# Softmax times V on one core: stores moved from SyncE's queue to GpSimd's, and the cast of V from GpSimd to VectorE

## The chip, the cores and the metric

The kernel runs on one core of one Trainium2 chip. A core has five engines that this text names by the profile's letters: PE (TensorE, matrix products, with PEld for its weight loads), DVE (VectorE), ACT (ScalarE), POOL (GpSimd) and SP (SyncE, which here only issues DMAs). Sixteen DMA engines move data between the chip's memory (HBM) and the core's on-chip memory (SBUF). The metric is the device time of one execution in microseconds (us); lower is better.

## The reference

For each of 8 x 12 = 96 heads there is a 1024 x 1024 float32 matrix of scores and a 1024 x 64 float32 matrix v. Softmax is taken along each row of the scores, and the result is multiplied by v.

```
batch, n_heads, seq, head_dim = 8, 12, 1024, 64
scores_max = np.max(scores, axis=-1, keepdims=True)
attn = np.exp(scores - scores_max)
attn = attn / (np.sum(attn, axis=-1, keepdims=True) + 1e-8)
return np.matmul(attn, v).astype(np.float32)
```

Of one head the scores are 4096 KB, v is 256 KB and the output is 256 KB.

## The kernel before, in words

A head is laid over 128 partitions: partition p holds 8 consecutive rows of the scores (R = 8, index r), 8 consecutive rows of v (C = 8, index c) and, later, 8 consecutive rows of the output. So a partition's share of a head is one run of 32 KB of scores, 2 KB of v and 2 KB of output in HBM.

The loop over heads n does this:

- `load(n)` issues two DMAs on SP: v into `v_sb` (L115), and the scores into `s_nat` (L120). The last head's scores come in four pieces of two rows each (1024 KB), all others in one piece. `v_pool` and `s_pool` have AHEAD = 4 buffers each. Loads of heads 0 to 3 are issued before the loop; `load(n + 4)` is issued in head n at r = 7 (L147).
- At the start of head n the 128 x 512 float32 `v_sb` is cast to float16 into one of three buffers `vones` (L130), on POOL. Each row of `vones` has a 65th element of 1.0, so that the same matrix product also gives the row sums of the softmax.
- For every second r, ACT takes the exponential of two rows per partition, 128 x 2048, from `s_nat` into the float16 tile `p_nat` (L136, four instructions for a head). No maximum is subtracted.
- For every r, PE transposes eight 128 x 128 blocks of `p_nat` into the PSUM tile `psT` (L140), and DVE copies that to SBUF as `pt` (L146).
- `finish` runs two r later (LAG = 2): eight matrix products of `pt` and `vones` add up in `psO` (L77, three PSUM buffers, each for four r). After four r, DVE takes the reciprocals of the row sums (L88) and multiplies (L89) into the tile `out_sb`, of which `ob_pool` has three. After r = 7 the head's `out_sb` goes to HBM in one DMA (L96), on SP.

All DMAs that SP issues are chained by `queue`, which makes the order of issue on SP that of the program's text: load of v, load of the scores, store, and so on. In the written order, the store of head n - 1 comes after `load(n + 3)` and before `load(n + 4)`. The order of instructions on the other engines is set by the framework's planner, which need not keep the written order: in the profile, both multiplications of L89 of a head come after that head's second reciprocal. The framework also puts in all waits.

Of the kernel before, what the change touches and what calls it, by code (L numbers as in the profile page):

```python
# [1 line left out]

# [5 lines left out]

FP32 = mybir.dt.float32
FP16 = mybir.dt.float16  # L10
EXP = mybir.ActivationFunctionType.Exp


@with_exitstack
def kernel(
    ctx: ExitStack,
    tc: tile.TileContext,
    scores: bass.AP,
    v: bass.AP,
    out: bass.AP,  # L20
):
    nc = tc.nc
    P = 128

    B, H, SQ, SK = scores.shape
    Bv, Hv, SKv, D = v.shape
    assert (B, H, SK) == (Bv, Hv, SKv)
    BH = B * H
    assert SQ % P == 0 and SK % P == 0
    R = SQ // P  # L30
    C = SK // P
    M = D + 1
    EB = 2
    G = 4
    LAG = 2
    NV = 3
    AHEAD = 4

    sc_bh = scores.rearrange("b h (p r) j -> (b h) p r j", p=P)
    v_bh = v.rearrange("b h (p c) d -> (b h) p c d", p=P)
    out_bh = out.rearrange("b h (p r) d -> (b h) p r d", p=P)

    const_pool = ctx.enter_context(tc.tile_pool(name="const", bufs=1))
    s_pool = ctx.enter_context(tc.tile_pool(name="spool", bufs=AHEAD))
    p_pool = ctx.enter_context(tc.tile_pool(name="ppool", bufs=6))
    v_pool = ctx.enter_context(tc.tile_pool(name="vpool", bufs=AHEAD))
    pt_pool = ctx.enter_context(tc.tile_pool(name="ptpool", bufs=5))
    ob_pool = ctx.enter_context(tc.tile_pool(name="obpool", bufs=3))  # L50
    rc_pool = ctx.enter_context(tc.tile_pool(name="rcpool", bufs=4))
    psT_pool = ctx.enter_context(tc.tile_pool(name="psTp", bufs=5, space=bass.MemoryType.PSUM))
    psO_pool = ctx.enter_context(tc.tile_pool(name="psOp", bufs=3, space=bass.MemoryType.PSUM))

    ident32 = const_pool.tile([P, P], FP32, name="ident32")
    make_identity(nc, ident32)
    ident16 = const_pool.tile([P, P], FP16, name="ident16")
    nc.vector.tensor_copy(out=ident16[:], in_=ident32[:])  # L58


    vones_bufs = []
    for k in range(NV):
        vo = const_pool.tile([P, C, M], FP16, name=f"vones{k}")
        nc.vector.memset(vo[:, :, D : D + 1], 1.0)  # L64
        vones_bufs.append(vo)

    pending = []

    def finish(u):

        n, r, pt, st = u
        g = r % G
        if g == 0:
            st["psO"] = psO_pool.tile([P, G, M], FP32, tag="psO", name="psO")
        psO = st["psO"]
        for c in range(C):
            nc.tensor.matmul(  # L77
                out=psO[:, g, :],
                lhsT=pt[:, c * P : (c + 1) * P],
                rhs=st["vones"][:, c, :],  # L80
                start=(c == 0),
                stop=(c == C - 1),
            )
        if g == G - 1:
            if r == G - 1:
                st["out_sb"] = ob_pool.tile([P, R, D], FP32, tag="out_sb", name="out_sb")
            recip = rc_pool.tile([P, G, 1], FP32, tag="recip", name="recip")
            nc.vector.reciprocal(out=recip[:], in_=psO[:, :, D : D + 1])  # L88
            nc.vector.tensor_tensor(  # L89
                out=st["out_sb"][:, r - G + 1 : r + 1, :],  # L90
                in0=psO[:, :, 0:D],
                in1=recip[:].to_broadcast([P, G, D]),
                op=mybir.AluOpType.mult,
            )
        if r == R - 1:
            queue(nc.sync.dma_start(out=out_bh[n], in_=st["out_sb"][:]))  # L96

    queued = []

    def queue(dma):  # L100

        if queued:
            tc.add_manual_dep(
                dma.ins,
                queued[-1].ins.name,
                mybir.DependencyInfo(mybir.DependencyClass.NoSync, mybir.DependencyReason.DATA),
                reason="queue order",
            )
        queued.append(dma)

    loaded = {}

    def load(n):
        v_sb = v_pool.tile([P, C, D], FP32, tag="v_sb", name="v_sb")
        queue(nc.sync.dma_start(out=v_sb[:], in_=v_bh[n]))  # L115
        s_nat = s_pool.tile([P, R, SK], FP32, tag="s_nat", name="s_nat")
        step = EB if n == BH - 1 else R
        for r in range(0, R, step):
            queue(
                nc.sync.dma_start(out=s_nat[:, r : r + step, :], in_=sc_bh[n, :, r : r + step, :])  # L120
            )
        loaded[n] = (s_nat, v_sb)

    for n in range(min(AHEAD, BH)):
        load(n)

    for n in range(BH):
        s_nat, v_sb = loaded.pop(n)
        vones = vones_bufs[n % NV]
        nc.gpsimd.tensor_copy(out=vones[:, :, 0:D], in_=v_sb[:])  # L130
        st = dict(vones=vones)

        for r in range(R):
            if r % EB == 0:
                p_nat = p_pool.tile([P, EB, SK], FP16, tag="p_nat", name="p_nat")
                nc.scalar.activation(out=p_nat[:], in_=s_nat[:, r : r + EB, :], func=EXP)  # L136
            p_row = p_nat[:, r % EB, :].rearrange("p (q c) -> p c q", c=C)
            psT = psT_pool.tile([P, SK], FP16, tag="psT", name="psT")
            for c in range(C):
                nc.tensor.transpose(  # L140
                    out=psT[:, c * P : (c + 1) * P],
                    in_=p_row[:, c, :],
                    identity=ident16[:],
                )
            pt = pt_pool.tile([P, SK], FP16, tag="pt", name="pt")
            nc.vector.tensor_copy(out=pt[:], in_=psT[:])  # L146
            if r == R - 1 and n + AHEAD < BH:  # L147
                load(n + AHEAD)
            pending.append((n, r, pt, st))
            if len(pending) > LAG:  # L150
                finish(pending.pop(0))
    while pending:
        finish(pending.pop(0))


# [1 line left out]
_INS = ['scores', 'v']  # L157
_OUTS = [((8, 12, 1024, 64), 'float32')]


# [23 lines left out]
```

## Time and profile before

| | |
|---|---|
| median of 3 runs | 1090.23 us (1089.81 to 1090.62) |
| profiled execution | 1090.23 us, its span 1088.4 us |
| mean granted TensorE clock | 0.813 |
| PE, PEld busy | 782.8 us (72%), 743.7 us (68%) |
| ACT busy | 704.0 us (65%) |
| DVE busy | 628.2 us (58%) |
| POOL busy | 60.1 us (6%), of which 59.4 us in 96 casts of L130 |
| read from and written to HBM | 427.82 MB and 25.17 MB, 416 GB/s over the span |

The span is the time from the first instruction to the last; the time of an execution is longer by 1.83 us. In the rows of a timeline the columns are the start in us from the span's start, the time in us, the engine, the line, the operation with its tiles and shapes, the number of instructions that are merged into the row, and in brackets the idle time ahead and what ended it. SPq is SP's queue of DMA issues: a row of it is an issue, not a transfer. In a table of windows each row is a stretch of time with the busy time of each engine, the granted clock, the mean busy share of the 16 DMA engines and the GB/s that they moved. The page's lines DMA and GB/s cut the span into 40 equal slices.

### The profile page before, as it was taken

How to read it: one execution, taken by the hardware profiler on the slowest of the kernel's cores; microseconds unless marked ns; L12 is line 12 of the kernel's file. 1: busy time of each engine (PE TensorE's matmuls, PEld its weight loads, DVE VectorE, ACT ScalarE, POOL GpSimd, SP SyncE). 2: the span in 40 equal slices, each digit the busy share in tenths (PEclk: the TensorE clock that was granted, in tenths of full speed). 3: DMA queues.
4: the chain of work that ended last, by engine and by line, in shares of the span. 5: the costliest groups of instructions: out<-in, count | busy, mean ns of one | idle time of the engine just before them, and what ended most of it. 6: DMA issues, size and time to landing. Idle time of an engine off the chain costs nothing.

```text
span 1088.4 us, 27687 instructions
## 1 busy us (share of the span) xinstructions
PE 782.8 (72%) x12288; PEld 743.7 (68%) x12288; DVE 628.2 (58%) x1156; ACT 704.0 (65%) x385; POOL 60.1 (6%) x102
## 2 busy tenths in 40 slices
PE   3767777676777767677776767777676777767676
PEld 3667667676766767677676767677676767767676
DVE  2556556565555655556565655655565565556555
ACT  4667576666757666665766666575665757566675
POOL 0000000000000000000000000000000000000000
PEclk9888878778787877878888887878888787787888
DMA  9999999999999999999999999999999999999994
GB/s 396 423 430 425 423 423 427 427 426 428 427 422 423 424 431 427 422 426 424 431 425 429 425 426 424 425 429 428 424 423 430 424 426 427 428 420 428 426 398 160
DMA packets 42024, 454.77 MB, mean 418 GB/s; under 512 B 4656, under 2 KB 4656, under 8 KB 29232
## 3 DMA queue, kind: packets, MB, share of 16 engines
q1 hardware_dynamic: 41904, 453.00, 98.5%
q8 instruction: 96, 1.57, 0.6%
q14 instruction: 24, 0.20, 0.0%
HBM read 427.82 MB, written 25.17 MB: 416 GB/s over the span
## 4 chain that ended last, share of the span: by engine, by line
DMA 96%; DVE 1%; PE 1%; issue 0%; SPq 0%; ACT 0%; DVEq 0%; ACTq 0%
DMA out_dram<-out_sb 69%; DMA s_nat<-in_scores_dram 18%; DMA v_sb<-in_v_dram 9%; DVE out_sb L89 1%; PE psT L140 1%; PE psO L77 0%; SPq L120 0%; ACT p_nat L136 0%; DVE pt L146 0%; SPq L115 0%; DVE recip L88 0%; DVEq L89 0%; SPq L96 0%; ACTq L136 0%
## 5 line engine op out<-in xcount | busy, mean ns | idle before, releaser
L136 ACT ACTIVATE p_nat<-s_nat 128x2048 f16<-128x2048 f32 x384 | 702.8, 1901 | 375.8 <-DMA s_nat<-in_scores_dram 364.7
L140 PE MATMUL psT<-ident,p_nat 128*128 128x128 f16 x6144 | 621.6, 264 | 274.5 <-ACT p_nat L136 273.5
L140 PEld LDWEIGHTS <-p_nat 128*128 128x128 f16 x6144 | 524.9, 155 | 301.5 <-ACT p_nat L136 295.2
L146 DVE COPY pt<-psT 128x1024 f16<-128x1024 f16 x768 | 529.0, 691 | 307.2 <-PE psT L140 285.4
L77 PE MATMUL psO<-vones,pt 128*128 128x65 f16 x6144 | 343.0, 204 | 27.3 <-DVE pt L146 26.3
L77 PEld LDWEIGHTS <-pt 128*128 128x128 f16 x6144 | 295.4, 107 | 39.2 <-DVE pt L146 38.3
L89 DVE TENSOR_TENSOR out_sb<-psO,recip 128x256 f32<-128x256 f32 x192 | 73.6, 420 | 98.7 <-DMA out_dram<-out_sb 98.6
L130 POOL CAST vones<-v_sb 128x512 f16<-128x512 f32 x96 | 59.4, 619 | 1007.3 <-DMA v_sb<-in_v_dram 995.5
L88 DVE RECIPROCAL recip<-psO 128x4 f32<-128x4 f32 x192 | 34.1, 178 | 49.9 <-PE psO L77 49.9
L136 ACT ACT_TABLE_LOAD x1 | 1.3, 1283 | 0.7 <-PEq L168 0.7
L64 DVE MEMSET vones<- 128x8 f16 x3 | 0.1, 65 | 0.8 <-PEq L168 0.8
L58 DVE CAST ident<-ident 128x128 f16<-128x128 f32 x1 | 0.2, 227 | 0.4 <-POOL ident masks.py:199 0.4
masks.py:199 POOL TENSOR_SCALAR_AFFINE_SELECT ident<-ident 128x128 f32<-128x128 f32 x1 | 0.3, 294 | 0.1
masks.py:197 POOL MEMSET ident<- 128x128 f32 x1 | 0.2, 205 | 0.3 <-POOLq L168 0.3
L168 POOL MEMSET const-float32-0.0<- 128x1 f32 x1 | 0.1, 99 | 0.2 <-issue 0.2
L168 POOL MEMSET const-bfloat16-1.0<- 128x1 bf16 x1 | 0.1, 102 | 0.0
L168 POOL MEMSET const-uint8-127<- 128x1 uint8 x1 | 0.1, 102 | 0.0
L168 POOL MEMSET const-float32-1.0<- 128x1 f32 x1 | 0.1, 99 | 0.0
## 6 DMA issues: line engine op xcount, KB each, us to landing
s_nat<-in_scores_dram SPq DMA_DIRECT2D x95, 4096.0 KB, 32.5
v_sb<-in_v_dram SPq DMA_DIRECT2D x96, 256.0 KB, 23.5
out_dram<-out_sb SPq DMA_DIRECT2D x96, 256.0 KB, 32.4
s_nat<-in_scores_dram SPq DMA_DIRECT2D x4, 1024.0 KB, 23.8
```

Source lines behind the costliest of these rows:

```text
L58: nc.vector.tensor_copy(out=ident16[:], in_=ident32[:])
L64: nc.vector.memset(vo[:, :, D : D + 1], 1.0)
L77: nc.tensor.matmul(out=psO[:, g, :], lhsT=pt[:, c * P : (c + 1) * P], rhs=st["vones"][:, c, :], start=(c == 0), stop=(c == C - 1),)
L88: nc.vector.reciprocal(out=recip[:], in_=psO[:, :, D : D + 1])
L89: nc.vector.tensor_tensor(out=st["out_sb"][:, r - G + 1 : r + 1, :], in0=psO[:, :, 0:D], in1=recip[:].to_broadcast([P, G, D]), op=mybir.Al ...
L130: nc.gpsimd.tensor_copy(out=vones[:, :, 0:D], in_=v_sb[:])
L136: nc.scalar.activation(out=p_nat[:], in_=s_nat[:, r : r + EB, :], func=EXP)
L140: nc.tensor.transpose(out=psT[:, c * P : (c + 1) * P], in_=p_row[:, c, :], identity=ident16[:],)
L146: nc.vector.tensor_copy(out=pt[:], in_=psT[:])
L168: nc = _bacc.Bacc("TRN2", target_bir_lowering=False, num_devices=1)
```

## The change

Two lines differ. The store of a head is issued by GpSimd instead of SP, and it is no longer part of the chain that `queue` makes, which now holds loads alone. The cast of v into `vones` is done by VectorE instead of GpSimd.

```
@@ finish @@
         if r == R - 1:
-            queue(nc.sync.dma_start(out=out_bh[n], in_=st["out_sb"][:]))
+            nc.gpsimd.dma_start(out=out_bh[n], in_=st["out_sb"][:])
...
@@ loop over heads @@
     for n in range(BH):
         s_nat, v_sb = loaded.pop(n)
         vones = vones_bufs[n % NV]
-        nc.gpsimd.tensor_copy(out=vones[:, :, 0:D], in_=v_sb[:])
+        nc.vector.tensor_copy(out=vones[:, :, 0:D], in_=v_sb[:])
         st = dict(vones=vones)
```

## The prediction

> **What bounds the kernel now.** I read the page's slices first, then the chain, then the timelines of ACT and SP, which show the chain's meaning.
>
> ```profile
> PE   3767777676777767677776767777676777767676
> DMA  9999999999999999999999999999999999999994
> GB/s 396 423 430 425 423 423 427 427 426 428 427 422 423 424 431 427 422 426 424 431 425 429 425 426 424 425 429 428 424 423 430 424 426 427 428 420 428 426 398 160
> q8 instruction: 96, 1.57, 0.6%
> ```
>
> The DMA engines are busy in every slice but the last and move 420 to 431 GB/s throughout, while no compute engine is above 72%. The chain of waits seems to say something else: it gives 69% of the span to the stores.
>
> ```profile
> DMA out_dram<-out_sb 69%; DMA s_nat<-in_scores_dram 18%; DMA v_sb<-in_v_dram 9%; DVE out_sb L89 1%; PE psT L140 1%; PE psO L77 0%; SPq L120 0%; ACT p_nat L136 0%; DVE pt L146 0%; SPq L115 0%; DVE recip L88 0%; DVEq L89 0%; SPq L96 0%; ACTq L136 0%
> ```
>
> ```profile
> DVE out_sb L89 <- DMA out_dram<-out_sb: 98.6, 91, 2.6
> ```
>
> A store takes 32.4 us from issue to landing because it stands behind about three heads of loads on SP's queue; the multiplications of L89 wait for the store three heads back to free its tile. That is a loop of waits which ends just in time, on engines with slack; the DMA engines work all the while. So taking this wait away (98.6 us of DVE idle time) is worth nothing by itself. What counts is how long a head takes on the DMA engines, and ACT's starts show it, since ACT starts a head when its scores land:
>
> ```profile
> 13.55 7.32 ACT L136 ACTIVATE p_nat<-s_nat 128x2048 f16<-128x2048 f32 x4 [11.54 <-DMA s_nat<-in_scores_dram]
> 23.94 7.32 ACT L136 ACTIVATE p_nat<-s_nat 128x2048 f16<-128x2048 f32 x4 [3.07 <-DMA s_nat<-in_scores_dram]
> ...
> 101.66 7.33 ACT L136 ACTIVATE p_nat<-s_nat 128x2048 f16<-128x2048 f32 x4 [3.71 <-DMA s_nat<-in_scores_dram]
> 112.67 7.32 ACT L136 ACTIVATE p_nat<-s_nat 128x2048 f16<-128x2048 f32 x4 [3.68 <-DMA s_nat<-in_scores_dram]
> 124.97 5.52 ACT L136 ACTIVATE p_nat<-s_nat 128x2048 f16<-128x2048 f32 x3 [4.99 <-DMA s_nat<-in_scores_dram]
> ```
>
> Heads 0 and 1 were issued before any store: 23.94 - 13.55 = 10.39 us for 4.456 MB, 429 GB/s. Later heads carry one store each: 112.67 - 101.66 = 11.01 us. A store on SP's queue therefore costs 0.62 us, 423 GB/s: its bytes at the common rate, no more. The next head took 12.30 us, 1.29 more; such steps come about every eight heads and I take them for the instruction packets of q8 (96 packets of 16 KB, 1.09 us each by their share of 0.6% of 16 x 1088.4 us), which another queue feeds. The end:
>
> ```profile
> 1043.38 0.33 SPq L115 DMA_DIRECT2D v_sb<-in_v_dram  x1
> 1044.10 11.26 SPq L120 DMA_DIRECT2D s_nat<-in_scores_dram  x4
> 1055.68 29.90 SPq L96 DMA_DIRECT2D out_dram<-out_sb  x5
> ```
>
> ```profile
> 1066.02 14.54 ACT L136 ACTIVATE p_nat<-s_nat 128x2048 f16<-128x2048 f32 x8 [4.24 <-DMA s_nat<-in_scores_dram]
> ```
>
> ```profile
> PE psO L77 <- DVE out_sb L89: 1.0, 1, 1.0
> ```
>
> The five last stores (91 to 95) are issued after all loads. Head 94's scores land at 1066.02; from there ACT runs heads 94 and 95 without a gap, and the span ends 22.4 us later.
>
> **The change, part by part.** I sum against the profiled execution, 1090.23 us (span 1088.4, 1.83 around it), which is also the median.
>
> *Issue of loads.* SP's waits show that each DMA waits for the landing of the one eight issues earlier: in a head, L115 waited for scores (89 times), L120 for a store (89), L96 for a v load (79). With three DMAs a head, eight are 2.7 heads in flight; with loads alone they would be four, until the buffers (AHEAD = 4) bind: the next scores go out when ACT has finished with a buffer, 7.3 us after a landing. Either way two heads or more, over 20 us of work, are always queued, so the DMA engines gain no work: 0 us. If that depth were gone, each head would pay the issue-to-start time; nothing in the change takes it away.
>
> *The cast.* 96 casts leave POOL, where each took 0.619 us, off the path (POOL waited 995.5 us for v). On DVE the nearest row is the 128x128 float32 cast, 0.227 us; four times the elements lies between 0.23 and 0.91 us, and I take 0.6. That is 96 x 0.6 = 58 us more for DVE, from 628 to 686 of 1088 us, or 7.1 us of 11.2 a head. Its place: v of head n + 1 lands 0.7 to 1.4 us after the scores of head n, while DVE has nothing until PE's first transposes of head n, 3.1 us after that landing (copy at 307.28, scores at 304.17). The cast is done by then: 0 us. Behind a waiting cast are the copies of L146, and PE waits for those; without this cover a late cast would move a head's work back, which four buffers of scores absorb, except at the end (rival 4). The next load of v waits for the cast now on DVE; 256 KB, two heads ahead, free.
>
> *The stores.* 96 issues leave SP (0.33 us each, in waiting time) and go to POOL, which has no other work left. (a) Order. On SP, the loads of head 94 have 90 stores ahead of them (0 to 89; then 90, then 91 to 95 after the last load). On its own queue, store n starts as soon as its head is done, about when the next head's scores land, and shares the engines with the load after that. So stores 90 to 92 now move before head 94 has landed, and the bound stream is three stores longer: 3 x 0.62 = +1.86 us. They used to move when the engines ran half empty. (b) The end. PE's single wait of 1.0 us for L89 (a `psO` buffer held because `out_sb` waited for store 91, queued behind the last loads) goes away: -1.0 us. What is late next is PE itself. (c) The last store is issued by POOL. No DMA of POOL is in the trace. From the last multiplication's end (1085.22) to the span's end are 3.2 us with SP; with POOL I bound the difference by 0 and 3.2 (twice as slow) and take one POOL operation, 0.6, as its software may need about that to start: +0.6 us. (d) The price of a store while another queue's loads run. This is the term that decides, and the trace doesn't hold it. Nearest rows: 0.62 us from ACT's starts (the store's tail under the next load), and 0.67 us from SP's: at 1021.11 the scores have landed, at 1021.77 and likewise at 304.84 (after 304.17) the store has, so 0.66 to 0.67 if its completion isn't covered. Far ends: 0 us, if a store out of SBUF could run entirely beside loads into SBUF; and 0.62 + 0.68, if switching queues costs what a q8 packet does (1.29 us for 16 KB, which is 0.61 at the common rate; one store is also 16 KB on each engine). Those give -59 and +65 us. I take the middle of the two near rows, 0.645, since the interleaved store has the same shape and bytes: 96 x 0.025 = +2.4 us.
>
> Sum: 1.86 - 1.0 + 0.6 + 2.4 = +3.9 us, so 1094.1 us.
>
> The Trainium skill, *DMA: Bandwidth & Descriptors*, section "Issuing engines are not separate DMA queues", says that DMAs of all issuing engines share the same 16 DMA engines and interleave, so that several issuers save only issue time. By it (d) would be 0 and the sum +1.5 us, 1091.7 us; no run here has yet shown two large queues at once.
>
> A rule that speaks against the change stands in *SBUF — State Buffer*, section "SBUF: two separate sides": GpSimd makes its own descriptors, through a port pair that VectorE locks while it copies from SBUF to SBUF in a fast mode. Here 768 of DVE's copies read PSUM, and the moved cast is the only such copy; by the rule a store would be held up by one cast at most, and with three `out_sb` tiles the sum is the same.
>
> **The rivals.** 1. *Two queues fill each other's gaps: faster.* If a share of each store runs beside the loads, a quarter say, a store costs 0.465 us: -14.9 + 1.5 gives 1076.8 us. It decides from a price below 0.58 us, where 96 x 0.04 = 3.7 us outweigh the 1.5 and the 0.2%. For it: 429 GB/s need not be the ceiling. Against: the rate with stores in the stream (11.01 us for 4.719 MB, 429 GB/s) equals that without, so mixing directions brought nothing. 2. *Switching is dear: much slower.* For it the q8 packets, 1.29 us for 0.61 us of bytes. If a store pays a tenth to a half of that surplus, 0.07 to 0.34 us, that is +6.5 to +33 us on the 1.5: 1098 to 1125 us. Against: those packets go to another place than HBM. 3. *It does nothing measurable*: price exactly 0.62, a POOL issue as quick as SP's, the ends cancel: 1090.2 to 1091.7 us. That the DMAs stay in effect in one stream is part of it. 4. *The cast lands in the wrong place in DVE's order*, a head early, and DVE stalls for a v that has not come: the loads go on, but at the end up to one head of PE work (782.8 / 96 = 8.2 us) is left over: up to 1102 us. Against: L89's place in before shows the planner counting with late DMAs.
>
> **How the numbers follow.** My sum, 1091.7 to 1096.5 us with the price between 0.62 and 0.67, gets 0.45; rival 1 0.15, rival 2 0.20, rival 3 0.13, rival 4 0.07. About 0.2%, 2.2 us, is what a measurement of this kernel can tell from no change: 1088.0 to 1092.4. Of my sum's case some 0.37 lies above that. So slower: 0.37 + 0.20 + 0.07 = 0.64; same: 0.08 + 0.13 = 0.21; faster: 0.15. The range leaves out the greater part of rival 1 below (0.10) and of rival 2 above (0.10): 1086 to 1108 us.
>
> **What would show it.** In the changed profile: heads still about 11.0 us apart on ACT (below 10.9 speaks for rival 1, above 11.1 for rival 2); DMA slices full; the wait of L89 for stores gone and the total little changed; a second large queue of some 25 MB; stores landing well under 32 us after issue; the last head but one landing 2 to 4 us later; DVE near 686 us with L146 waiting for PE as before. The prediction is wrong if ACT's spacing moves by more than 0.1 us, if a head's L146 waits for v, or if the tail after the last landing differs from 22.4 us by more than 2 us.

## The result, and the profile after

The changed kernel takes 1094.79 us in the median of 4 runs (1094.51 to 1095.15), the kernel before 1090.26 us (1089.81 to 1090.62, 4 runs). The ratio is 1.0042 with a 95% interval of 1.0025 to 1.0059: slower by 0.4%. The forecast was 1094.1 us, slower. The sum was right to 0.7 us, but, as the profile shows at once, not by the steps that made it up: the transfers did not cost more but a little less, and the loss is a cost of some 6 us at the very end that the prediction put at 0.6 us.

The profiled execution took 1095.15 us, its span is 1093.4 us, 5.0 us longer than before. The page's GB/s by slice, its queues, and its rows for the moved operations (POOLq is POOL's queue of instructions, as SPq is SP's):

```profile
GB/s 394 428 430 426 429 427 425 424 426 431 425 432 423 423 429 426 426 429 428 429 421 430 425 424 433 422 432 425 424 427 421 435 423 424 428 425 428 428 363 93
q1 hardware_dynamic: 28080, 427.83, 92.0%
q0 software_dynamic: 7680, 25.17, 5.7%
L96 POOL DMA_DIRECT2D out_dram<-out_sb x96 | 54.7, 570 | 1028.7 <-DVE out_sb L89 1028.7
L130 DVE CAST vones<-v_sb 128x512 f16<-128x512 f32 x96 | 41.1, 428 | 47.1 <-DMA v_sb<-in_v_dram 46.4
```

The second queue is there: q0 carries the 25.17 MB of stores, and a store now lands 10.7 us after its issue (32.4 us before). The rate is what it was, until it falls off earlier in the last two slices. POOL spends 0.57 us on issuing a store, and the cast takes DVE 0.43 us.

The starts of ACT, for the stretch and the end that the prediction showed (columns as in the timelines of before):

```profile
102.59 7.32 ACT L136 ACTIVATE p_nat<-s_nat 128x2048 f16<-128x2048 f32 x4 [3.67 <-DMA s_nat<-in_scores_dram]
113.58 7.32 ACT L136 ACTIVATE p_nat<-s_nat 128x2048 f16<-128x2048 f32 x4 [3.67 <-DMA s_nat<-in_scores_dram]
...
1053.91 7.32 ACT L136 ACTIVATE p_nat<-s_nat 128x2048 f16<-128x2048 f32 x4 [3.79 <-DMA s_nat<-in_scores_dram]
1064.89 14.53 ACT L136 ACTIVATE p_nat<-s_nat 128x2048 f16<-128x2048 f32 x8 [3.66 <-DMA s_nat<-in_scores_dram]
```

Heads are still 10.99 us apart, but head 94's scores land at 1064.89 us, 1.13 us *earlier* than the 1066.02 of before. Then the end, by the timelines of DVE and POOL, first of the kernel before and then of the changed one:

```profile
1084.80 0.42 DVE L89 TENSOR_TENSOR out_sb<-psO,recip 128x256 f32<-128x256 f32 x1
```

```profile
1083.43 0.42 DVE L89 TENSOR_TENSOR out_sb<-psO,recip 128x256 f32<-128x256 f32 x1
1084.15 0.54 POOL L96 DMA_DIRECT2D out_dram<-out_sb  x1 [4.98 <-DVE out_sb L89]
```

The last multiplication ends at 1083.85, 1.4 us earlier than before (1085.22). Yet the span ends at 1093.4, 9.55 us after it, against 3.18 us before. What fills this time stands in the list of instructions that belong to no line of the kernel but to its end (the launch line, 179). Minimum, median and longest in ns are followed by the first and the last start, and the longest DRAIN is the first; first the kernel before, then the changed one:

```profile
L179 POOLq DRAIN  x3: 34/78/696, 1067.3 to 1088.1; - x3
```

```profile
L179 POOLq DRAIN  x3: 45/102/8472, 1084.1 to 1093.1; - x3
```

POOL's queue ends with a DRAIN. Before, it took 0.70 us and began at 1067.3, together with POOL's last cast, with 20 us to spare. Now it takes 8.47 us and can begin only when POOL has issued the last store: 1084.13 + 8.47 = 1092.60, and 0.8 us later the span is over. The last bytes of the store are in memory at 1086.1 by the records of its packets, so 6.5 us of the DRAIN come after all work is done.

So the 5.0 us of span are: -1.13 (head 94's scores) - 0.24 (from there to the last multiplication, 18.96 us against 19.20) + 6.37 (from there to the end).

Two more views. The waits: the line of L89 for stores is gone (98.6 us of before), and SP now waits mostly for ACT to free a buffer of scores:

```profile
SPq L120 <- ACT p_nat L136: 680.7, 92, 7.4
SPq L120 <- DMA s_nat<-in_scores_dram: 276.8, 93, 8.4
```

And the chain of the changed kernel, which shows what a chain can hide:

```profile
issue 87%; POOL 5%; DMA 5%; PE 1%; ACT 1%; DVE 0%; POOLq 0%; SPq 0%; ACTq 0%
```

The chain followed back from POOL's DRAIN finds POOL's store issues and, between them, time for which it has no cause ("issue"). It is a list of what POOL did, not of what bounds the kernel; the starts of ACT and the end are better guides.

### The profile page after: what moved, and what is told of

It reads as the page before. It is cut to its first block, busy times and chain, and to the rows that moved or that the text cites. A ratio compares the mean times of both kernels' runs of the same rounds, so it can differ in the third digit from the quotient of the medians.

```text
span 1093.4 us, 27493 instructions
## 1 busy us (share of the span) xinstructions
PE 784.1 (72%) x12288; PEld 745.6 (68%) x12288; DVE 656.1 (60%) x1252; ACT 704.0 (64%) x385; POOL 55.4 (5%) x102
## 3 DMA queue, kind: packets, MB, share of 16 engines
q0 software_dynamic: 7680, 25.17, 5.7%
HBM read 427.82 MB, written 25.17 MB: 414 GB/s over the span
## 4 chain that ended last, share of the span: by engine, by line
issue 87%; POOL 5%; DMA 5%; PE 1%; ACT 1%; DVE 0%; POOLq 0%; SPq 0%; ACTq 0%
POOL out_dram L96 5%; DMA s_nat<-in_scores_dram 5%; ACT p_nat L136 1%; PE psT L140 1%; PE psO L77 0%; DVE pt L146 0%; DVE out_sb L89 0%; POOLq L96 0%; DVE recip L88 0%; POOLq L179 0%; SPq L115 0%; ACTq L136 0%
## 5 line engine op out<-in xcount | busy, mean ns | idle before, releaser
L146 DVE COPY pt<-psT 128x1024 f16<-128x1024 f16 x768 | 527.5, 690 | 326.4 <-PE psT L140 313.2
L96 POOL DMA_DIRECT2D out_dram<-out_sb x96 | 54.7, 570 | 1028.7 <-DVE out_sb L89 1028.7
L89 DVE TENSOR_TENSOR out_sb<-psO,recip 128x256 f32<-128x256 f32 x192 | 80.6, 420 | 3.3
L130 DVE CAST vones<-v_sb 128x512 f16<-128x512 f32 x96 | 41.1, 428 | 47.1 <-DMA v_sb<-in_v_dram 46.4
## 6 DMA issues: line engine op xcount, KB each, us to landing
out_dram<-out_sb POOLq DMA_DIRECT2D x96, 256.0 KB, 10.7
```

Of the source, the lines that this page charges most:

```text
L89: nc.vector.tensor_tensor(out=st["out_sb"][:, r - G + 1 : r + 1, :], in0=psO[:, :, 0:D], in1=recip[:].to_broadcast([P, G, D]), op=mybir.Al ...
L96: nc.gpsimd.dma_start(out=out_bh[n], in_=st["out_sb"][:])
L130: nc.vector.tensor_copy(out=vones[:, :, 0:D], in_=v_sb[:])
```

## The experiments

The theory after the result, A: the stream of transfers is not slower but about 1 us shorter at head 94, and the loss is the DRAIN at POOL's end. The rival, B: the cost lies in the transfers, and the end is a fixed price. Four kernels, timed together with the kernel before (1090.04 us), take the change apart. The kernels further below were timed with it again (1090.10 and 1089.82 us), and each ratio is to its runs of the same time.

**The last two stores on SP.** In the changed kernel:

```
         if r == R - 1:
-            nc.gpsimd.dma_start(out=out_bh[n], in_=st["out_sb"][:])
+            if n >= BH - 2:
+                queue(nc.sync.dma_start(out=out_bh[n], in_=st["out_sb"][:]))
+            else:
+                nc.gpsimd.dma_start(out=out_bh[n], in_=st["out_sb"][:])
```

> The changed kernel, but the stores of the last two heads (94 and 95) are issued by SP. Theory A (end): 6.4 us of the slowdown stand after the last multiplication, where POOL's DRAIN of 8.47 us begins when POOL has issued its last store. Then this DRAIN starts some 13 to 18 us earlier, is over before the last store has landed, and the span ends 3.2 us after the last multiplication as in the kernel before: span 1087.0 us, time 1088.8 us (1088.0 to 1089.6), below the kernel before. Theory B (stream): the cost lies in the transfers, the end is a fixed price of having used POOL's queue at all and comes after everything else: 1094.8 us as with the change.

Measured: 1088.65 us, ratio to before 0.9988 (0.9979 to 0.9997). The DRAIN at the end and the last steps of ACT and DVE (lines have moved by three):

```profile
L182 POOLq DRAIN  x3: 45/235/10497, 1066.0 to 1086.6; - x3
1064.84 14.53 ACT L139 ACTIVATE p_nat<-s_nat 128x2048 f16<-128x2048 f32 x8 [3.67 <-DMA s_nat<-in_scores_dram]
1082.89 0.42 DVE L89 TENSOR_TENSOR out_sb<-psO,recip 128x256 f32<-128x256 f32 x1
```

The DRAIN is even longer, 10.5 us, but starts at 1066.0 and is over at 1076.5, under the work of the last head. The span of 1086.9 us ends 3.6 us after the last multiplication. Two issues moved out of 96 turn a kernel that is 0.4% slower into one that is 0.1% faster: A holds, B falls.

**Each half of the change alone.** Stores on POOL with the cast left on POOL; and the cast on DVE with the stores left on SP (each is one line of the change's diff).

> Only the stores move to POOL; the cast of v stays on POOL. Theory A: the cast is worth nothing on either engine, so 1094.8 us (1094.0 to 1095.6), with the long DRAIN at the end. Rival: the cast on DVE delays copies and is part of the loss: then this is 1 us or more faster than the change.

> Only the cast of v moves to DVE; all stores stay on SP. Theory A: 1090.2 us (1089.5 to 1091.0), the same as before, with the short DRAIN of POOL. Rival (cast costs on DVE): 1091 us or more.

Measured: 1095.02 us (ratio 1.0046, 1.0034 to 1.0059) with the stores alone, and 1089.84 us (1.0000, 0.9991 to 1.0008) with the cast alone. Head 94's scores landed at 1065.00 us in the first and at 1065.55 us in the second. The whole effect is that of the stores; the place of the cast shows no effect. It also gives a second reading of the landing with stores on SP: 1066.02, 1065.55 and (next kernel) 1065.83, on average 1065.8 us, against 1064.89, 1064.84 and 1065.00 us, on average 1064.9 us, with stores on POOL.

**Only the last store on POOL**, in the kernel before:

```
-            queue(nc.sync.dma_start(out=out_bh[n], in_=st["out_sb"][:]))
+            if n == BH - 1:
+                nc.gpsimd.dma_start(out=out_bh[n], in_=st["out_sb"][:])
+            else:
+                queue(nc.sync.dma_start(out=out_bh[n], in_=st["out_sb"][:]))
```

> The kernel before, with only the store of the last head (95) issued by POOL. Theory A: one store by POOL at the very end is enough for the whole price of the end: the span ends 9.5 us after the last multiplication in place of 3.2, so 1090.2 + 6.4 = 1096.6 us (1095.8 to 1097.4), and heads land as before. Rival C: the DRAIN grows with the number of stores that POOL has issued (8.47 us for 96): then with one store it is near the 0.7 us of before and the time is 1090 to 1091.5 us.

```profile
L182 POOLq DRAIN  x3: 40/99/2535, 1085.1 to 1088.3; - x3
```

Measured: 1090.55 us, ratio 1.0004 (0.9995 to 1.0013). My own expectation missed: one store at the end is not enough. The span ends 3.8 us after the last multiplication, 0.6 us later than with SP. POOL's DRAIN takes 2.54 us, which is about the time the store needs to land (2.4 us), so rival C was right so far: a long DRAIN needs more than one store issued by POOL.

**Half of the stores on POOL** (heads 48 to 95; `if n < BH // 2` chooses SP):

> Stores of heads 0 to 47 on SP in the chain, of heads 48 to 95 on POOL; the rest as in the changed kernel. How long is POOL's DRAIN at the end? It took 8.47 us after 96 stores and 2.54 us after one (which is about the time that this one store took to land). Theory C (the DRAIN grows with the number of stores POOL has issued, 8.47 / 96 = 0.088 us each): 48 x 0.088 = 4.2 us, the span ends some 5.4 us after the last multiplication, and the time is about 1091 us (1090.3 to 1091.8). Rival S (a step: 8.5 us as soon as more than a few have been issued): DRAIN 8.5 us, time 1095 us. Rival L (the DRAIN lasts until the last store has landed): 2.5 us, 1089.5 us.

```profile
L182 POOLq DRAIN  x3: 40/93/4556, 1085.0 to 1090.1; - x3
1066.27 14.54 ACT L139 ACTIVATE p_nat<-s_nat 128x2048 f16<-128x2048 f32 x8 [3.80 <-DMA s_nat<-in_scores_dram]
```

Measured: 4.56 us of DRAIN, between those for 1 and for 96 stores. So where the last store is issued at the very end, the DRAIN is longer the more stores POOL has issued: by the records of the packets it goes on for 0.4, 2.6 and 6.5 us after the last byte has landed. From 48 to 96 stores that is (8.47 - 4.56) / 48 = 0.082 us a store, but this is no rule for other cases. The kernels below that leave the last stores to SP have DRAINs of 10.5 us (94 stores), 14.15 us (91) and 14.67 us (84): there POOL's last store stands beside loads and lands 6 to 11 us after the DRAIN has begun, and the DRAIN goes on for 4.0 to 4.4 us more. What sets its length stays open. What the runs show is when it begins, and so whether it is hidden. The time, 1092.22 us (ratio 1.0020, 1.0012 to 1.0029), is 0.4 us above what I allowed, because I had forgotten the transfers: head 94 landed at 1066.27, later than with all stores on SP or all on POOL. That is used below.

**Why are the transfers faster?** With stores on POOL, three more stores (90 to 92) have moved when head 94's scores land, and still they land 0.9 us earlier. The starts of ACT for earlier heads show where this comes from (us; the last two rows are kernels of this section and the one above):

| stores | head 9 | head 47 | head 60 | head 93 | head 94 |
|---|---|---|---|---|---|
| all on SP, or all but the last (mean of three) | 112.42 | 538.44 | 684.67 | 1054.15 | 1065.80 |
| on POOL, or all but the last two (mean of three) | 113.55 | 539.02 | 684.94 | 1053.92 | 1064.91 |
| on ACT, issued late | 113.46 | 538.93 | 685.02 | 1054.00 | 1065.01 |
| heads 48 to 95 on POOL | 112.31 | 538.32 | 686.36 | 1055.15 | 1066.27 |

The stores on POOL begin with a loss of 1.13 us, as they move earlier, and make it good evenly: 1.36 us from head 9 to head 93, 0.016 us a head. That agrees with the heads' spacing, 10.99 us in place of 11.01, where a head without a store takes 10.39: a store costs 0.60 us in place of 0.62. Another 0.66 us come in the last step alone: with stores on SP, head 94 starts 11.57 to 11.70 us after head 93, with stores on POOL 10.98 or 10.99. What makes that step longer isn't shown.

The next runs ask whether it is the greater number of loads in flight (D), POOL's larger packets (P: 25.17 MB in 7680 packets, where SP's stores went in 2 KB pieces) or a queue of their own (Q). All start from the kernel with the last two stores on SP.

*AHEAD = 3* (one line):

> The kernel with the last two stores on SP, with AHEAD = 3: three buffers of scores and of v, so fewer loads in flight (time from issue to landing some 26 us in place of 36.9). Theory D (the greater number of loads in flight is what made the stream faster): head 94 lands 1 to 3 us later than 1064.8, time 1090 to 1092 us. Theories Q and P (the store's own queue or packets): head 94 at 1064.8 as with AHEAD = 4, time 1088.65 us (1088.0 to 1089.4).

```profile
1064.51 14.54 ACT L139 ACTIVATE p_nat<-s_nat 128x2048 f16<-128x2048 f32 x8 [3.56 <-PE psO L77]
```

Measured: 1088.77 us (ratio 0.9988, 0.9979 to 0.9997), head 94 at 1064.51, though a load of scores is in flight for 25.7 us in place of 36.9. D falls, and with it any worth of the deeper queue of loads.

*Stores on ACT's queue* (`nc.scalar` in place of `nc.gpsimd`):

> Stores 0 to 93 issued by ACT instead of POOL, stores 94 and 95 by SP (as in the kernel with the last two stores on SP, whose 1088.65 us is the comparison). The question is why the scores of head 94 land at 1064.8 to 1065.0 us with POOL's stores, while the same loads with stores in SP's queue land at 1065.6 to 1066.0, although three more stores have moved by then. Theory Q (a queue of its own is what helps): ACT's stores are also in another queue than the loads, so head 94 lands at 1064.9 again and the time is 1088.7 us (1088.0 to 1089.5). Theory P (POOL's packets of 4 KB in place of 2 KB are what helps): ACT's stores go in 2 KB packets, price 0.62 us as on SP, so head 94 lands at 1065.8 + 1.9 = 1067.7 and the time is 1091.5 us. Both: if ACT's stores make it wait for DVE ahead of the next head's exponential, up to 1 us comes on top at the end.

```profile
ACT p_nat L139 <- DVE vones L133: 429.5, 93, 5.1
```

Measured: 1160.12 us (1.0643, 1.0628 to 1.0657). It told nothing of Q and P, since it changed something else: the planner put the issue of a head's store ahead of the next head's exponentials, so ACT waited there for DVE to finish the head before (the wait names the cast that DVE has then begun; the store's issue at 311.12 us follows the end of L89 at 311.08), and a head took as long as its way through ACT, PE and DVE, 11.5 to 12.4 us. The same queue again, with each store held until the following head's exponentials are issued:

```
                 last_exp = nc.scalar.activation(out=p_nat[:], in_=s_nat[:, r : r + EB, :], func=EXP)
+                if r == R - EB and late:
+                    m, t = late.pop(0)
+                    dma = nc.scalar.dma_start(out=out_bh[m], in_=t[:])
+                    tc.add_manual_dep(dma.ins, last_exp.ins.name, ...)
```

> Stores 0 to 93 on ACT's queue again, but each is issued only after the exponentials of the following head (out_sb has five buffers), so ACT no longer waits for DVE ahead of an exponential; stores 94 and 95 on SP. About 92.4 stores have then moved before head 94's scores land, against 90 in the kernel before (landing at 1065.8 on average). Theory P (packets: 2 KB on ACT as on SP, 0.62 us a store): 1065.8 + 2.4 x 0.62 = 1067.3 us for head 94 (1066.7 to 1067.8), time 1091.1 us. Theory Q (a queue of its own makes a store cost 0.59 us): 1065.8 - 90 x 0.62 + 92.4 x 0.59 = 1064.5 us, time 1088.3 us. ACT should again wait for the scores and not for DVE.

```profile
q10 hardware_dynamic: 13536, 24.65, 5.9%
1065.01 1.91 ACT L140 ACTIVATE p_nat<-s_nat 128x2048 f16<-128x2048 f32 x1 [3.69 <-DMA s_nat<-in_scores_dram]
```

Measured: 1088.63 us (0.9989, 0.9980 to 0.9998), head 94 at 1065.01. The packets are small again (13536 for 24.65 MB), and ACT waits for scores. P asked for 1067.3 and 1091.1, Q for 1064.5 and 1088.3, and the table's row for it follows POOL's: a queue of their own, and not the size of the packets, is what makes the stores cheaper. What the DMA engines do better then, the trace doesn't show.

*The loads of v on POOL, too* (`nc.gpsimd.dma_start` for `v_sb`, outside the chain):

> The kernel with the last two stores on SP, and the loads of v also issued by POOL (not in SP's chain): the software queue carries twice the bytes, 190 DMAs, and q1 holds scores and two stores alone. Theory P (the software queue's larger packets are what made a store cheaper, 0.59 us in place of 0.62): v becomes cheaper by the same 0.03 us a head, 2.9 us in all, head 94 lands near 1062 and the time is 1085.8 us. Theory Q (a store beside loads in its own queue overlaps them): v is a load like the scores, nothing is gained, 1088.65 us. Theory C adds that POOL's DRAIN takes 190 x 0.088 = 16.7 us; POOL issues its last DMA near 1066, so it ends near 1083 and is still hidden.

```profile
POOL v_sb L118 <- DVE vones L133: 922.0, 90, 15.1
DVE out_sb L89 <- DMA out_dram<-out_sb: 284.6, 81, 5.8
```

Measured: 1106.73 us (1.0135, 1.0114 to 1.0157), and nothing learnt on packets. POOL works in order: the load of v waits for the cast that frees its buffer, the store behind it on POOL waits along, L89 waits for the store, and so the loop of waits of the kernel before is back, now with work of DVE inside it. Its DRAIN took 7.49 us after 190 DMAs where 16.7 were expected; so a fixed price for each DMA fails here, too.

**Is term (a) real: does a store ahead of head 94 cost its bytes at the end?** Three kernels hold stores back until SP has issued all loads: the last five (91 to 95) on SP in the changed kernel; the last twelve (84 to 95) likewise; and the same twelve in the kernel before. `out_sb` gets 6, 14 and 14 buffers. The twelve are kept in a list that is emptied after the last load:

```
+    def flush():
+        if BH - 1 in issued:
+            while held:
+                m, t = held.pop(0)
+                queue(nc.sync.dma_start(out=out_bh[m], in_=t[:]))
...
+            if n >= BH - HOLD:
+                held.append((n, st["out_sb"]))
+                flush()
+            else:
                 nc.gpsimd.dma_start(out=out_bh[n], in_=st["out_sb"][:])
...
         loaded[n] = (s_nat, v_sb)
+        issued.append(n)
+        flush()
```

> The changed kernel with the stores of the last five heads (91 to 95) issued by SP, that is behind all loads in SP's queue, and six buffers of out_sb so that nothing waits for them. Term (a) of the prediction says that each store that moves before head 94's scores puts them off by its price. Against the kernel with the last two on SP, stores 91 and 92 no longer do: 2 x 0.59 = 1.2 us less, head 94 at 1063.6, time 1087.4 us (1086.7 to 1088.1). If term (a) is not real: 1088.65 us.

> As before, with 12 stores (84 to 95) held back until SP has issued the last load, and 14 buffers of out_sb; stores 0 to 83 by POOL. 84 stores ahead of head 94 in place of 93: 9 x 0.59 = 5.3 us less than with the last two on SP, head 94 at 1059.5, time 1083.3 us (1082.4 to 1084.4), below the kernel before by 0.6%. If term (a) is not real: 1088.65 us.

> The kernel before (stores on SP, cast on POOL), with the same 12 stores held back until the last load is issued and 14 buffers of out_sb. 84 stores ahead of head 94 in place of 90: 6 x 0.62 = 3.7 us, head 94 at 1062.1; the wait of PE for a psO buffer at the end goes too, 0.6 us: time 1085.8 us (1085.0 to 1086.8). The difference to the kernel with POOL's stores and the same 12 held back is then 84 x 0.03 = 2.5 us, the price of POOL's larger packets once more.

ACT's start for head 94, in the order of the three kernels:

```profile
1063.66 14.53 ACT L139 ACTIVATE p_nat<-s_nat 128x2048 f16<-128x2048 f32 x8 [3.02 <-DMA s_nat<-in_scores_dram]
```

```profile
1059.34 14.53 ACT L151 ACTIVATE p_nat<-s_nat 128x2048 f16<-128x2048 f32 x8 [3.05 <-DMA s_nat<-in_scores_dram]
```

```profile
1061.34 14.54 ACT L151 ACTIVATE p_nat<-s_nat 128x2048 f16<-128x2048 f32 x8 [3.04 <-DMA s_nat<-in_scores_dram]
```

| | time, us | ratio to before | head 94 at, us | stores ahead of it |
|---|---|---|---|---|
| last two on SP | 1088.65 | 0.9988 (0.9979 to 0.9997) | 1064.84 | 93 |
| last five on SP | 1087.04 | 0.9975 (0.9966 to 0.9984) | 1063.66 | 91 |
| twelve held back, others on POOL | 1082.68 | 0.9939 (0.9925 to 0.9952) | 1059.34 | 84 |
| twelve held back, all on SP | 1084.91 | 0.9956 (0.9943 to 0.9968) | 1061.34 | 84 |

Term (a) is real. From 93 stores to 91 the landing moves by 1.18 us, 0.59 us a store, and from 93 to 84 by 5.50 us, 0.61 us a store. From 90 to 84 on SP (1065.8 to 1061.34) it moves by 4.5, 0.74 us a store; there the longer last step of 11.6 us has gone, too. The greater number of `out_sb` buffers is not what helps: up to the heads whose stores are held back nothing changes (head 84 starts at 953.38 us with twelve held back on SP, at 953.80, 953.21 and 953.54 us in the three kernels of the table's first row above). The two kernels with twelve held back differ by 2.0 us at the landing and 2.2 us in time, with the same stores ahead: the worth of a queue of their own, and on average 2.0 / 84 = 0.024 us a store. The last words of the expectation above put this down to POOL's packets; the run with stores on ACT speaks against that. The third kernel of the table is the fastest of this study: 0.6% below the kernel before.

## Why the prediction was right, and where it was not

By its own test the prediction's working failed: it named a tail that differs from 22.4 us by more than 2 us as a sign of being wrong, and from head 94's landing to the end of the span there are now 28.5 us. Another of its signs failed, too: head 94's scores were to land 2 to 4 us later and landed 1.13 us earlier. The total came out by luck: two errors of 5 to 6 us, in (c) and (d), cancel.

- *Bound, loads, cast.* Right. Heads stay 11.0 us apart, taking away 98.6 us of L89's waits gained nothing by itself, more loads in flight are worth 0 (AHEAD = 3 shows it), and the cast is worth nothing that can be measured. It took 0.43 us, below the 0.6 that I took; DVE is busy for 656 us and not 686.
- *(a) Order, +1.86 us.* Right as a mechanism and near in size: 0.59 and 0.61 us a store with the others on POOL, and 0.74 on SP, the last step included.
- *(b) PE's wait at the end, -1.0 us.* The wait is gone, but from head 94's landing to the last multiplication only 0.24 us were saved. Mis-sized. The granted clock in this stretch was 0.82 before and after. In the kernels with the last two stores on SP and with half on POOL it was 0.91, and the stretch took 18.5 us, 0.7 us less than before; so no profile shows the 1.0 us. Why it is less isn't shown.
- *(c) The last store on POOL, +0.6 us.* This is the step that failed. It measured +6.37 us, outside its bounds of 0 and 3.2 us. I bounded the cost of *issuing* a store by POOL and landing it, and both are indeed small (0.54 us; with one store at the end the kernel took 0.5 us more in all). The cost that came is in POOL's own end, a DRAIN that the trace of before shows with 0.70 us, hidden under the last head. I read only the operations of the kernel's lines and not those of its end. What makes the DRAIN long stays open.
- *(d) The price of a store beside loads, +2.4 us.* Wrong in sign. I took the middle of 0.62 and 0.67; measured was about 0.60. Three stores more, by (a) 1.86 us, and a landing 0.9 us earlier make some 2.8 us to explain: 1.36 us come evenly from head 9 to head 93, 0.66 us in the step to head 94, and the rest ahead of head 9, where the earlier stores cost 1.13 us and not 1.86. Half the stores on POOL confirm that the even part goes by the store: the switch at head 48 puts the loads off (1.69 us against the first row of the table at head 60), and from head 60 to head 93 they gain 0.69 us again, 0.021 us a head. So rival 1's cheaper store is there, but small: 0.016 to 0.024 us a store, where it needed more than 0.04 to decide. That two queues fill each other's gaps, its reason, isn't shown. Rival 2 (switching is dear) falls: it would have shown as heads further apart. Rival 4 didn't come: DVE's L146 waits for PE (313.2 us), as before.

With the measured terms the sum is 1.86 - 2.8 - 0.24 + 6.37 = +5.2 us, against 5.0 in the span. That is no second proof, since -2.8 was worked out from (a) and the landings.

The Trainium skill, *DMA: Bandwidth & Descriptors*, section "Issuing engines are not separate DMA queues", says that DMAs of all issuers interleave on the same 16 engines and that several issuers save only issue time. The rows agree nearly: one store costs 0.60 us in a queue of its own and 0.62 us in the loads' queue. The 0.02 us go beyond the sentence, and with 84 stores they are 2 us. The rule that VectorE's fast copies from SBUF to SBUF hold up GpSimd's descriptors (*SBUF — State Buffer*, "SBUF: two separate sides") didn't show in the time: with the cast on DVE or on POOL it is 1094.79 or 1095.02 us, and an issue on POOL takes 0.57 or 0.54 us.

## What to carry to other kernels

When a queue is moved to another engine, read that engine's last instructions too: an engine's end can cost more than its last operation (here 8.47 us after an issue of 0.54 us), and it starts only after the last thing that the engine issues. Two of 96 stores, left on the old queue, were worth 6 us here. In a kernel that is bound by its loads, every store that moves before the last loads puts off the end by its own bytes; hold the last ones back until all loads are issued. Five on SP in place of two gained 1.6 us here and twelve 6.0 us; how many more would pay wasn't tried. And a sum that comes out right is no proof of its terms: compare them one by one with the stretches of the new profile.

## What the runs showed of the hardware that I had not expected

- POOL's DRAIN at the kernel's end takes 0.7 us in the kernel before, without DMAs of POOL. Where POOL's last store is the kernel's last, it takes 2.54 us after 1 store of 256 KB, 4.56 us after 48 and 8.47 us after 96. Where that store stands beside loads it takes 10.5 to 14.7 us after 84 to 94, and after 190 DMAs, half of them loads of v, it took 7.49 us.
- A store of 256 KB costs the loads' stream about 0.62 us in the loads' own queue and about 0.60 us in another, whether that queue is POOL's with 4 KB packets or ACT's with 2 KB packets.
- Digits of the DMA busy share are coarse: with stores on ACT ahead of the exponentials, the DMA line showed 9 in every slice but the last, as ever, while the rate was down from 418 to 393 GB/s on average and ACT was waiting for DVE.
